# Other places in SBUF for the weights of five stretches of float32r products, a later START in mLSTM, and first weight copies on VectorE in layer 1

## The chip, the cores and the metric

The kernel runs on one core of one Trainium2 chip, in one launch. The metric is the device time of that launch in microseconds; lower is better. The core's engines are TensorE (PE, with its weight loads shown apart as PEld), VectorE (DVE), ScalarE (ACT), GpSimd (POOL) and SyncE (SP), which issues most DMA transfers.

## The reference

The reference runs four mixer layers of width 1024 over 256 tokens: two transformer layers, each with a squared-ReLU MLP, then an mLSTM mixer and a sparse-attention (NSA) mixer. Everything is float32.

```python
for layer in range(2):                      # first_block
    h = rms_norm(x, g_mix[layer])
    x = x + (even_mixer(h, ...) if layer == 0 else odd_mixer(h, ...))
    h = rms_norm(x, g_mlp[layer])
    u = einsum("bsd,df->bsf", h, w_up[layer])          # 1024 -> 4096
    x = x + einsum("bsf,fd->bsd", square(relu(u)), w_down[layer])
# second_block
x = x + mlstm_mixer(rmsnorm(x, ml_norm), ...)   # w_in 1024 -> 4096, w_out 2048 -> 1024
x = x + nsa_mixer(rmsnorm(x, nsa_norm), ...)
return rmsnorm(x, final_norm)
```

Nearly all arithmetic is in the products with the weight matrices (`w_in`, `w_out`, `w_up`, `w_down`). In the mLSTM the input projection feeds a short convolution, from which values and gates are made; in layer 1 (`odd_mixer`) 16 heads attend causally with a forget gate.

## The kernel before

**Weights in chunks.** All weight matrices are packed into one DRAM tensor of 137 chunks, each 128 partitions by 2048 float32 (1 MB), and used in order. For each chunk, `prepare` starts the DMA into `wraw` on SyncE's queue and cuts it into two float32r parts: ScalarE copies it rounded into `whi` (L124), VectorE writes the rest, `wraw - whi`, into `wlo` (L127), in halves of 1024 columns. The activations are cut the same way into pairs (`xh`, `xl`; `hh`, `hl`; `yh`, `yl`). A float32 product is then three float32r products: high by high, low by high, high by low. The ring holds three buffers of each of `wraw`, `whi` and `wlo`; two chunks are prepared ahead of the one in use (one ahead in part of layer 1).

**Two ways of multiplying.** In `gemm_tok_steps` (L199 to L201) the activations are the stationary operand, loaded with LDWEIGHTS, and a chunk's columns move, 512 at a time (256 in chunk 2): the output has tokens on the partitions. In `bank_add` (L239, L241, L242) a 128 x 128 block of the chunk is stationary and 256 tokens of the activations move; a chunk gives 16 blocks and 48 products. `gemm_feat`, `out_proj_steps`, `mlp` and the input and output projections of the mLSTM all go through `bank_add`.

**Where the operands lie.** `chunk_tiles` allocates `whi` and `wlo` aligned to LINE = 256 bytes, with SHIFT = 48 spare elements. Chunks in TOK, those that `gemm_tok_steps` uses, start 48 elements (192 bytes) into the tile, all others at 0. The activations' tiles come from `late`, which puts them 192 bytes past a multiple of 256. Chunk numbers by use: 9 to 12 layer 0's output, 13 to 28 its MLP up, 29 to 44 down; 57 to 60 layer 1's output, 61 to 76 up, 77 to 92 down; 93 to 108 mLSTM's input, 109 to 116 its output; the rest is layer 0's and layer 1's input and NSA.

**Breaks in the stream.** Between two runs of products others come in: after each MLP's up half `norm_end` (L299) makes the sum of squares, and `rstd_row` (L314) spreads the reciprocal over the partitions with four small products, a few products into the down half.

**mLSTM.** Here the order of TensorE's instructions is the order of the code (`manual_schedule`). Loop step i of `order` does `gemm_feat` of chunk 93 + i, in 8 blocks k of six products; `between[i][k]` holds what is put in ahead of block k. From step 2 on the finished banks are worked up on VectorE and ScalarE: `x_tiles` evacuates into `xi` (L761, two buffers, begun by a memset at L760), convolves (L772) and writes `xc` (L775). For each pair of x tiles, `values` (L783, 16 small products of `xi` with `bdv`) and `gates` (L790, products of `xc` and `xi`) go into TensorE's stream together. For the first pair the place is START = (4, 2): chunk 97, ahead of block 2; for the second pair (6, 4). The `bdv` tiles, two buffers, are loaded from POOL's queue (L763).

**Layer 1.** `causal_heads` works through four head pairs: scores (L515, L519), softmax (VectorE L467, ScalarE L470, VectorE L478 and L485), then `weights_T` transposes the weights on TensorE (L499) and copies them out of PSUM into `pt` (L501) with `nc.any`, which lets the scheduler choose between VectorE and ScalarE, and `pv` multiplies with the values (L528). Products of the next group's projection are put in between as fills. Only layer 1 passes `extra` to `causal_heads`.

The order of all other instructions on each engine is the scheduler's; `issue_after` holds the VectorE cuts behind some chains.

Of the kernel before, what the change touches and what calls it, by code (L numbers as in the profile page):

```python
# [10 lines left out]
F32R = mybir.dt.float32r  # L11
# [6 lines left out]
P = 128  # L18
# [7 lines left out]
PTBUFS = 2  # L26

LAG = (2, 4)
START = (4, 2)
WARM = 3  # L30
RAW = (125, 126)

TOK = {*range(9), *range(45, 57), *range(117, 121), 123, 124, 127, 128, 135, 136}


LINE = 256
SHIFT = 48
PSUM = dict(s=2, t=2, o=1)


# [31 lines left out]
def late(pool, shape, name):  # L72

    n = int(np.prod(shape))
    t = pool.tile([P, SHIFT + n], F32R, name=name, tag=name, bufs=1, align_bytes=LINE)[:, SHIFT:]
    names = "abcdefg"[:len(shape)]
# [3 lines left out]
class Builder:  # L80
# [11 lines left out]
    def begin(self):  # L92
# [4 lines left out]
        with self.tc.tile_pool(name="warm", bufs=1) as pool:  # L97
            z = pool.tile([P, 512], F32, name="zero", tag="zero")
            nc.vector.memset(z, 0.0)
            ps = self.pa.tile([P, 512], F32, name="t", tag="t", bufs=PSUM["t"])  # L100
            for i in range(WARM):
# [13 lines left out]
        self.chunk_no = 2  # L115

    def chunk_tiles(self):
        at = SHIFT if self.chunk_no in TOK else 0
        parts = [self.ring.tile([P, 2048 + SHIFT], F32R, name=n, tag=n, bufs=3, align_bytes=LINE)[:, at:at + 2048]
                 for n in ("whi", "wlo")]  # L120
        return [self.ring.tile([P, 2048], F32, name="wraw", tag="wraw", bufs=3)] + parts

# [29 lines left out]
    def single(self, tag, shape=(P, 512)):  # L152
        pool = self.pr if tag == "s" else self.pa
        return pool.tile(list(shape), F32, name=tag, tag=tag, bufs=PSUM[tag])

# [138 lines left out]
    def norm_end(self, kind, tag="t"):  # L294

        nc = self.nc
        ps = self.pa.tile([P, 512], F32, name=tag, tag=tag, bufs=PSUM[tag])
        for b in range(2):
# [10 lines left out]
    def rstd_row(self, scale=1.0):  # L309

        nc = self.nc
        ps = self.pa.tile([P, 512], F32, name="t", tag="t", bufs=PSUM["t"])
        for b in range(2):
# [93 lines left out]
    def transposed(self, t, c0, n):  # L407

        nc = self.nc
        ps = self.pa.tile([P, 2, T], F32, name="t", tag="t", bufs=PSUM["t"])  # L410
        for i in range(n):
# [75 lines left out]
            self.chain = last  # L487
        return Ls

    def weights_T(self, pool, Ls):  # L490

        nc = self.nc
        out = []

        for w, parts in ((P, (2,)), (T, (0, 1))):
            ps = self.pa.tile([P, 2, w], F32, name="t", tag="t", bufs=PSUM["t"])
            for e in range(2):
                for j, i in enumerate(parts):
                    nc.tensor.transpose(ps[:, e, j * P:(j + 1) * P], Ls[e][:, i * P:(i + 1) * P], self.ident)  # L499
            pt = pool.tile([P, 2, w], F32, name="pt", tag=f"pt{w}", bufs=PTBUFS)  # L500
            nc.any.tensor_copy(pt, ps)  # L501
            out.insert(0, pt)
        return out

# [26 lines left out]
    def causal_heads(self, pool, qk, v, vcol, tables, yh, yl, npair, extra=None, sinks=None, fills=(0, 0, 0, 0)):  # L531
        def weights(p):
            s = self.scores(qk(p), [extra(2 * p + e) for e in range(2)] if extra else None)
            kw = dict(hold=extra is not None)
            if sinks is not None:
                kw.update(nsinks=sinks[0][:, 2 * p:2 * p + 2], sinks=sinks[1][:, 2 * p:2 * p + 2])
            return self.softmax(pool, s, [tables(2 * p + e) for e in range(2)], **kw)

        ahead = [weights(0)]
        for p in range(npair):  # L540
            if p + 1 < npair:
                self.fill(fills[0])
                ahead.append(weights(p + 1))
            self.fill(fills[1 if p == 0 else 2])
            pts = self.weights_T(pool, ahead.pop(0))
            self.fill(fills[3])
            o = self.pa.tile([P, 512], F32, name="o", tag="o", bufs=PSUM["o"])
            self.pv(o, pts, v(), [vcol(p, e) for e in range(2)], True, True)
            self.split(yh[:, p], yl[:, p], o[:, :T])
# [179 lines left out]
    def mlstm(self):  # L729
# [3 lines left out]
        with tc.tile_pool(name="ml", bufs=2) as pool:  # L733
# [69 lines left out]
            with tc.manual_schedule(engines={PE}):  # L803
# [4 lines left out]
                for i, n in enumerate(order):  # L808
# [3 lines left out]
                    for n, p in ps:  # L812
                        if n is None:
                            z_tiles(i // 3, p)
                        else:

                            pair += x_tiles(n, p)
                            if n % 2:
                                at = max((order.index(n) + LAG[0], LAG[1]), START if n < 2 else (0, 0))
                                between[at[0]].setdefault(at[1], []).extend(pair[::2] + pair[1::2])  # L820
# [591 lines left out]
```

## Time and profile before

| | |
|---|---|
| timed runs | 945.35, 947.33 and 2352.52 us; median 947.33 us |
| the profiled execution | 939.13 us, of which its span (first to last instruction) 937.4 us |
| mean granted TensorE clock | 0.999 of 2.4 GHz |
| TensorE busy | 921.9 us, 98% of the span |
| VectorE, ScalarE busy | 692.2 us (74%), 553.6 us (59%) |
| DMA | 152.55 MB, mean 163 GB/s |

Busy time of TensorE counts a product from its start to its end, and products overlap: the next one starts before the last one's results are out. So the duration of a product (276 ns, say) is not what it costs; that is the distance from its start to the next start. Times of rows are microseconds from the span's start.

### The profile page before, as it was taken

How to read it: one execution, taken by the hardware profiler on the slowest of the kernel's cores; microseconds unless marked ns; L12 is line 12 of the kernel's file. 1: busy time of each engine (PE TensorE's matmuls, PEld its weight loads, DVE VectorE, ACT ScalarE, POOL GpSimd, SP SyncE). 2: the span in 40 equal slices, each digit the busy share in tenths (PEclk: the TensorE clock that was granted, in tenths of full speed). 3: DMA queues.
4: the chain of work that ended last, by engine and by line, in shares of the span. 5: the costliest groups of instructions: out<-in, count | busy, mean ns of one | idle time of the engine just before them, and what ended most of it. 6: DMA issues, size and time to landing. Idle time of an engine off the chain costs nothing.

```text
span 937.4 us, 17579 instructions
## 1 busy us (share of the span) xinstructions
PE 921.9 (98%) x7096; PEld 843.7 (90%) x7096; DVE 692.2 (74%) x1510; ACT 553.6 (59%) x1028; POOL 6.8 (1%) x16
## 2 busy tenths in 40 slices
PE   9999999999999999999999999999999999999997
PEld 6777999999998777899999999899888998888986
DVE  6997866655557787998664556978778878778994
ACT  7767656544445675566554444556645456379883
POOL 0000000000000000000000000000000000000000
PEclk9999999999999999999999999999999999999999
DMA  8723455555554342365555555544411555341311
GB/s 308 300 91 135 166 207 211 182 184 186 192 196 170 124 167 90 136 223 204 201 180 189 210 186 192 191 147 163 141 69 45 180 194 180 135 180 47 113 46 45
DMA packets 22609, 152.55 MB, mean 163 GB/s; under 512 B 2608, under 2 KB 2736, under 8 KB 4992
## 3 DMA queue, kind: packets, MB, share of 16 engines
q1 hardware_dynamic: 21744, 148.44, 44.8%
q0 software_dynamic: 784, 2.98, 0.9%
q8 instruction: 56, 0.92, 0.4%
q14 instruction: 25, 0.20, 0.1%
HBM read 150.36 MB, written 1.05 MB: 162 GB/s over the span
## 4 chain that ended last, share of the span: by engine, by line
PE 86%; DVE 6%; ACT 5%; issue 1%; DMA 1%; SPq 0%; ACTq 0%; DVEq 0%
PE g L239 19%; PE g L242 19%; PE g L241 19%; PE g L199 4%; PE g L200 4%; PE g L201 4%; DVE wlo L127 2%; PE o L528 2%; PE t L499 2%; ACT L L470 1%; ACT whi L124 1%; PE s L1140 1%; PE s L199 1%; PE s L200 1%; PE s L201 1%
## 5 line engine op out<-in xcount | busy, mean ns | idle before, releaser
L127 DVE TENSOR_TENSOR wlo<-wraw,whi 128x1024 fp32r<-128x1024 f32 (+1 forms) x274 | 324.1, 1204 | 123.7 <-ACT whi L124 123.1
L124 ACT ACTIVATE whi<-wraw 128x1024 fp32r<-128x1024 f32 (+1 forms) x274 | 277.8, 1042 | 217.9 <-PE g L241 118.3
L242 PE MATMUL g<-xh,wlo 128*128 128x256 f32 x928 | 260.3, 280 | 0.0
L239 PE MATMUL g<-xh,whi 128*128 128x256 f32 x928 | 259.0, 279 | 0.0
L241 PE MATMUL g<-xl,whi 128*128 128x256 f32 x928 | 258.5, 279 | 0.0
L239 PEld LDWEIGHTS g<-xh,whi 128*128 128x128 f32 x928 | 174.6, 188 | 2.2 <-issue 0.9
L242 PEld LDWEIGHTS g<-xh,wlo 128*128 128x128 f32 x928 | 174.6, 188 | 0.8 <-issue 0.2
L241 PEld LDWEIGHTS g<-xl,whi 128*128 128x128 f32 x928 | 174.4, 188 | 0.2
L239 PE MATMUL g<-hh,whi 128*128 128x256 f32 x512 | 142.8, 279 | 0.0
L242 PE MATMUL g<-hh,wlo 128*128 128x256 f32 x512 | 142.8, 279 | 0.0
L241 PE MATMUL g<-hl,whi 128*128 128x256 f32 x512 | 142.6, 279 | 0.0
L242 PEld LDWEIGHTS g<-hh,wlo 128*128 128x128 f32 x512 | 97.2, 190 | 0.0
L239 PEld LDWEIGHTS g<-hh,whi 128*128 128x128 f32 x512 | 96.1, 188 | 0.0
L241 PEld LDWEIGHTS g<-hl,whi 128*128 128x128 f32 x512 | 96.1, 188 | 0.0
L199 PE MATMUL g<-whi,xh 128*128 128x512 f32 x176 | 71.5, 406 | 0.4 <-ACT xh L279 0.3
L200 PE MATMUL g<-wlo,xh 128*128 128x512 f32 x176 | 70.0, 397 | 0.0
L201 PE MATMUL g<-whi,xl 128*128 128x512 f32 x176 | 68.8, 394 | 0.0
L470 ACT ACTIVATE L<-L,nm 128x128 f32<-128x128 f32 (+1 forms) x128 | 56.6, 449 | 13.0 <-DVE nm L467 12.9
L239 PE MATMUL g<-yh,whi 128*128 128x256 f32 x224 | 63.5, 284 | 0.0
L242 PE MATMUL g<-yh,wlo 128*128 128x256 f32 x224 | 62.8, 280 | 0.0
L241 PE MATMUL g<-yl,whi 128*128 128x256 f32 x224 | 62.6, 279 | 0.0
L239 PEld LDWEIGHTS g<-yh,whi 128*128 128x128 f32 x224 | 42.1, 188 | 1.4 <-issue 1.4
(354 smaller groups left out, 1373.3 us busy)
## 6 DMA issues: line engine op xcount, KB each, us to landing
wraw<-in_w SPq DMA_DIRECT2D x135, 1024.0 KB, 4.9
wraw<-in_w SPq DMA_DIRECT2D x4, 512.0 KB, 7.2
tabs<-in_tabs SPq DMA_DIRECT2D x2, 1024.0 KB, 8.9
xT<-in_x SPq DMA_DIRECT2D x4, 256.0 KB, 7.3
bdv<-in_bdv POOLq DMA_DIRECT2D x8, 128.0 KB, 2.9
mlw<-in_mlw POOLq DMA_DIRECT2D x1, 992.0 KB, 6.9
nq<-in_gf POOLq DMA_DIRECT2D x1, 512.0 KB, 3.9
out_y<-nqr SPq DMA_DIRECT2D x2, 256.0 KB, 2.1
```

The lines of the kernel that those rows point to most:

```text
L124: self.nc.scalar.activation(hi[:, s], w[:, s], AF.Copy)
L127: self.nc.vector.tensor_tensor(lo[:, s], w[:, s], hi[:, s].bitcast(F32), op=ALU.subtract)
L199: nc.tensor.matmul(ps[b][:, :n], xh, hi[:, sl], start=kt == 0, stop=False)
L200: nc.tensor.matmul(ps[b][:, :n], xh, lo[:, sl], start=False, stop=False)
L201: nc.tensor.matmul(ps[b][:, :n], xl, hi[:, sl], start=False, stop=kt == KT - 1)
L239: nc.tensor.matmul(o, hi[:, s], ah, start=bank["new"], stop=False)
L241: nc.tensor.matmul(o, hi[:, s], al, start=False, stop=False)
L242: nc.tensor.matmul(o, lo[:, s], ah, start=False, stop=last and j == 1 and i == len(acts) - 1)
L470: nc.scalar.activation(Ls[i][:, c], Ls[i][:, c], AF.Exp, bias=nm[:, b, i:i + 1], scale=-1.0, accum_out=den[:, b, i:i + 1])
L499: nc.tensor.transpose(ps[:, e, j * P:(j + 1) * P], Ls[e][:, i * P:(i + 1) * P], self.ident)
L528: nc.tensor.matmul(o[64 * e:64 * e + 64, kt * P:T], v[:, kt, c0[e]:c0[e] + 64], pts[kt][:, e], start=start and kt == 0, stop=stop and kt == 1)
L1140: nc.tensor.matmul(ps, q[:, b * P:(b + 1) * P], kst[:, g, e, o, :, :P + b * P], start=o == 0, stop=o == 1)
```

## The change

`START` goes from (4, 2) to (4, 7). `whi` and `wlo` get ROOM = 64 spare elements instead of 48, and chunks in five ranges start 56, 60, 4, 52 or 40 elements into their tile instead of at 0; TOK chunks stay at 48 and all others at 0. In layer 1, the first head pair (p = 0) of each of the two groups has its copies out of PSUM on VectorE by name instead of `nc.any`.

```diff
-START = (4, 2)
+START = (4, 7)
...
+ROOM = 64
+
+PLACES = ((range(10, 29), 56), (range(29, 45), 60), (range(59, 77), 4), (range(77, 95), 52), (range(110, 117), 40))
...
     def chunk_tiles(self):
-        at = SHIFT if self.chunk_no in TOK else 0
-        parts = [self.ring.tile([P, 2048 + SHIFT], F32R, name=n, tag=n, bufs=3, align_bytes=LINE)[:, at:at + 2048]
+        at = SHIFT if self.chunk_no in TOK else sum(n for chunks, n in PLACES if self.chunk_no in chunks)
+        parts = [self.ring.tile([P, 2048 + ROOM], F32R, name=n, tag=n, bufs=3, align_bytes=LINE)[:, at:at + 2048]
                  for n in ("whi", "wlo")]
...
-    def weights_T(self, pool, Ls):
+    def weights_T(self, pool, Ls, by=None):
...
-            nc.any.tensor_copy(pt, ps)
+            (by or nc.any).tensor_copy(pt, ps)
...
-            pts = self.weights_T(pool, ahead.pop(0))
+
+            pts = self.weights_T(pool, ahead.pop(0), self.nc.vector if extra is not None and p == 0 else None)
```

## Rows read from the trace of the kernel before

**Rows 1.** The page: busy time of each engine; engines' shares of the last chain.
```profile
PE 921.9 (98%) x7096; PEld 843.7 (90%) x7096; DVE 692.2 (74%) x1510; ACT 553.6 (59%) x1028; POOL 6.8 (1%) x16
...
PE 86%; DVE 6%; ACT 5%; issue 1%; DMA 1%; SPq 0%; ACTq 0%; DVEq 0%
```

**Rows 2.** Waits of TensorE, whole span: us in total, times, longest us.
```profile
PE o L790 <- DVE xc L775: 2.1, 1, 2.1
...
PE o L528 <- ACT pt L501: 0.9, 1, 0.9
```

**Rows 3.** L239 in six stretches: count, duration ns min/median/max, first and last start.
```profile
L239 PE MATMUL g<-xh,whi x192: 276/276/276, 122.9 to 187.8; 128*128 128x256 f32 x192
...
L239 PE MATMUL g<-hh,whi x223: 281/281/281, 200.9 to 279.3; 128*128 128x256 f32 x112
...
L239 PE MATMUL g<-xh,whi x240: 276/276/276, 405.5 to 486.8; 128*128 128x256 f32 x120
...
L239 PE MATMUL g<-hh,whi x224: 276/276/276, 499.0 to 574.8; 128*128 128x256 f32 x112
...
L239 PE MATMUL g<-xh,whi x15: 281/281/281, 728.3 to 733.2; 128*128 128x256 f32 x15
...
L239 PE MATMUL g<-yh,whi x63: 276/276/276, 746.4 to 767.5; 128*128 128x256 f32 x63
```

**Rows 4.** Timeline of TensorE, both MLPs' down halves: start, length, instruction, count.
```profile
194.98 0.63 PE L314 MATMUL t<-cst,nr 128*128 128x128 f32 x4
...
493.63 0.63 PE L314 MATMUL t<-cst,nr 128*128 128x128 f32 x4
```

**Rows 5.** L199 in layer 1 as in rows 3, and timeline of chunk 2.
```profile
L199 PE MATMUL g<-whi,xh x16: 389/389/395, 285.3 to 295.5; 128*128 128x512 f32 x16
...
20.10 0.28 PE L201 MATMUL s<-whi,xl 128*128 128x256 f32 x1
...
20.70 0.28 PE L200 MATMUL s<-wlo,xh 128*128 128x256 f32 x1
```

**Rows 6.** Timeline of mLSTM's scores; groups by form: L519's busy us, mean ns.
```profile
673.19 1.89 PE L896 MATMUL s<-xc,yk 128*128 128x256 f32 x8
...
L519 PE MATMUL s<-negc,selr 64*128 64x384 f32 x16 | 2.7, 335 | 0.0
```

**Rows 7.** Timeline of TensorE around the first and the second pair of x tiles.
```profile
604.81 1.95 PE L783 MATMUL s<-bdv,xi 128*128 128x128 f32 x16
...
609.93 0.39 PE L239 MATMUL g<-xh,whi 128*128 128x256 f32 x1
...
622.76 1.95 PE L783 MATMUL s<-bdv,xi 128*128 128x128 f32 x16
...
625.07 0.38 PE L790 MATMUL o<-xc,W 128*8 128x256 f32 x1
...
625.62 0.38 PE L239 MATMUL g<-xh,whi 128*128 128x256 f32 x1
```

**Rows 8.** Timeline of VectorE and POOL there; in brackets idle time and releaser.
```profile
608.65 0.68 DVE L775 SCALAR_TENSOR_TENSOR xc<-cu,cv 128x512 f32<-128x512 f32 x1
609.26 0.68 DVE L761 TENSOR_TENSOR xi<-g,row 128x512 f32<-128x512 f32 x1
...
610.11 0.06 DVE L760 MEMSET xi<- 128x6 f32 x1 [0.16 <-PE o L790]
...
622.25 0.68 DVE L775 SCALAR_TENSOR_TENSOR xc<-cu,cv 128x512 f32<-128x512 f32 x1
...
606.16 0.54 POOL L763 DMA_DIRECT2D bdv<-in_bdv  x1 [24.05 <-PE s L783]
```

**Rows 9.** Timeline of ScalarE and VectorE in layer 1, both groups' first pair.
```profile
334.68 0.84 ACT L501 COPY pt<-t 128x256 f32<-128x256 f32 x2
...
334.82 0.18 DVE L478 RECIPROCAL inv<-den 128x4 f32<-128x4 f32 x1 [1.12 <-ACT L L470]
...
375.26 1.01 DVE L501 COPY pt<-t 128x256 f32<-128x256 f32 x2
```

## The prediction

> **What bounds the kernel now.** I read the page first. TensorE is busy for 921.9 of 937.4 us, and 86% of the chain that ended last is TensorE's own [rows 1]. So time can go in two ways only: TensorE waits less, or its products follow each other faster. The granted clock is 0.999 of 2.4 GHz over the whole span, so no clock is to be won. Second, the waits of TensorE: the two longest are 2.1 us for VectorE in mLSTM (L790) and, after one at the very start, 0.9 us for ScalarE in layer 1 (L528) [rows 2]; they lie where the change's two other edits are. Third, the pace of the products, which "busy" hides because they overlap. I took it from the first and last start of L239 in long unbroken stretches: L239 is every third product of a bank, so the pitch from start to start is the stretch divided by three times the count less one.
>
> The reader is to see two paces for the same instruction [rows 3]. Layer 0's mlp, up: (187.8 - 122.9)/(3 x 191) = 113.3 ns. Its down half: (279.3 - 200.9)/(3 x 222) = 117.7 ns. Layer 1's mlp: up (486.8 - 405.5)/(3 x 239) = 113.4, down (574.8 - 499.0)/(3 x 223) = 113.3. mLSTM's output: the first weights (733.2 - 728.3)/(3 x 14) = 116.7, the later ones (767.5 - 746.4)/(3 x 62) = 113.4. The durations tell the same without rounding: 281 ns at the slow pace and 276 at the quick one, minimum, median and maximum alike, while VectorE, ScalarE and DMA work beside them. The step of about 4.4 ns is no noise of other engines.
>
> The two down halves are the same code on the same shapes, with their weights at the same remainder. The rows show nothing that sets them apart: the same four small L314 products break in soon after the start, for 0.63 us each time [rows 4]. One run comes out of that at the slow pace and one at the quick pace, and each keeps it to its end. I read this as two reads of TensorE, the moving operand and the next weights, that interfere or not by their phase and by where they begin. That is argued from the two paces; no row shows an address.
>
> **The change, part by part.** *Places.* `chunk_tiles` puts `whi` and `wlo` of 78 chunks at 224, 240, 16, 208 or 160 bytes past a multiple of 256 instead of at 0 (56, 60, 4, 52, 40 elements of 4 bytes); each chunk is 48 products, 3744 in all. No instruction is added, and the writes of ScalarE and VectorE and the DMA keep their sizes: the chunks in TOK sit 192 bytes off already and are written by the same two lines. The tiles grow from 2096 to 2112 elements, exactly 33 x 256 bytes; as each is aligned to 256, I take the slots as unmoved, at no cost.
>
> What can it give? Slow now among those chunks are the down half of layer 0 (16 chunks, 768 products) and one chunk at the head of mLSTM's output (48). At 4.4 ns each that is 816 x 4.4 = 3.6 us, if the new places hold the quick pace everywhere. Nothing hides it, since TensorE sets the pace, and nothing else falls late by it: ScalarE and VectorE are busy for 59% and 74% of the span [rows 1].
>
> Is there a third pace below 113.3? No row shows one. The 512-wide products take (295.5 - 285.3)/(3 x 15) = 226.7 ns, the same 0.443 ns per column at another place and with the operands' roles swapped; the 256-wide ones of chunk 2 take (20.70 - 20.10)/5 = 120 ns [rows 5]. The products of L519 read one column for all their weights, so the place of their own weights can't matter: duration less pitch is 162.7 ns at the quick pace (276 - 113.3) and 162.3 for the wide ones (389 - 226.7), so their 335 ns mean 172 ns for 384 columns, 0.449 each [rows 6]. From below the nearest row is plain float32: L896 does 256 columns in two passes in (1.89 - 0.38)/7 = 0.216 us, 108 ns a pass [rows 6]. I take 113.3 as the floor, since every float32r row stands there or above, and keep 108 and 120 as bounds.
>
> The Trainium skill speaks against this edit. By "TensorE: Matmul & The Clock Gate", section "Step-by-step: what each phase is for", TensorE has two independent read ports, and loading the next weights steals no bandwidth from the running product. By that rule a place changes nothing and this term is 0 instead of 3.6 us. The two paces of one instruction don't agree with it as it stands.
>
> *mLSTM, START (4,2) to (4,7).* The values and gates of the first two x tiles now stand ahead of chunk 97's last block instead of its third: 30 products later, 30 x 0.1133 = 3.4 us, so L783 starts at 604.81 + 3.4 = 608.2 [rows 7]. In the second pair the last gates come 625.07 - 622.76 = 2.3 us after the first L783, so here at 610.5; what they wait for ends at 608.65 + 0.68 = 609.3 [rows 7, 8]. The wait goes. The block took 609.93 - 604.81 = 5.1 us; it will take the second pair's 625.62 - 622.76 = 2.9, so 2.2 less.
>
> What is late next: the gates also free `xi`. VectorE began the third tile at 609.26 and the fourth after a wait for L790 at 610.11 [rows 8]; now the first buffer is free only at about 610.5, 1.2 us later, and behind that memset on VectorE queue the evacuation, the convolution and the cuts of two chunks. The second pair stays at (6,4). TensorE reaches it 2.2 us sooner, so its last gates want `xc` at 625.07 - 2.2 = 622.9. VectorE makes it at 622.25 + 0.68 = 622.9 if nothing moved and at 624.1 if all of the 1.2 us comes through. So 0 to 1.2 us come back as a wait at the second pair. Net gain 1.0 to 2.2; I take 1.3, nearer the low end, as VectorE runs almost without a pause there. POOL's two transfers of `bdv` wait for L783 [rows 8] and follow it by 3.4 us; their tiles are wanted at the second pair, over 10 us later. Chunk 100's weights wait for chunk 97's last product, and that comes earlier.
>
> *Layer 1, the first copies of weights on VectorE.* In the first group ScalarE does both copies, from 334.68 for 0.84 us, behind its exponentials, and TensorE waits 0.9 [rows 2, 9]. VectorE stands idle for 1.12 us before 334.82. Its own two copies in the second group take 1.01 us [rows 9]: started at 333.7 they end at 334.7, about when L528 would begin without its wait. Gain 0.85 at best. If the reciprocal and the scalings are put ahead instead, the copies end about 2 us later and it costs 1.3. In the second group VectorE does them already, so nothing changes there. I take 0.7.
>
> **Sum.** 3.6 + 1.3 + 0.7 = 5.6 us. From the profiled execution's 939.1 us that gives 933.5. The timed runs are at 945.35 and 947.33, 6 to 8 us above it. The one thing seen here that can differ by whole microseconds from run to run is the pace that a stretch falls into: 18 chunks (layer 1's output and up, or layer 1's down with mLSTM's first two) at the slow pace are 864 x 4.4 = 3.8 us, two such stretches 7.6. If that is the 6 to 8 us, places that hold the pace take them too, and the median also comes to about 934; if it is anything else, the median becomes 947.3 - 5.6 = 941.7. I say 934.
>
> **Rivals.** *The places do nothing*, and a run's pace depends on its phase alone: only 2.0 us go, 945 by the median, 937 by the profile. For it: one place, 0, shows both paces. Against: chunk 2 has another place and another pace. It is what the section of the Trainium skill named above would give.
>
> *A third pace.* At plain float32's 108 ns, 2928 products gain 5.3 and 816 gain 9.7 ns: 23.4 us, with the waits 25.4: 914 from the profile, 922 from the median. For it: the pass at 108. Against: no float32r product in the rows. It alone would make over 2%.
>
> *The new places are worse.* Chunk 2's 120 ns shows that some relation of the two operands is slower still. At 120 everywhere, 2928 x 6.7 + 816 x 2.3 = 21.5 us, less the waits 19.5: 959 from the profile, 967 from the median. The sign turns once one stretch of 18 chunks falls there (864 x 6.7 = 5.8 us, the whole sum). Against: five places would have to be bad for a clear loss.
>
> *The wait returns at the second pair in full*, VectorE then setting mLSTM's first third: 0.3 more than in my sum. It lies inside my range.
>
> **How the numbers follow.** "Faster" and "slower" mean by over 2%, about what a measurement here can tell from no change: below 928.4 or above 966.3. Quick pace held and the waits mostly gone: 0.58, between 931 and 942. Places do nothing: 0.16, 937 to 946. Third pace, whole or on some runs: 0.17, 914 to 930. Worse places: 0.09, 945 to 968. Faster takes the third pace and a sliver of the first case: 0.18. Slower needs nearly the whole of the worse places: 0.04. Same: 0.78. For 8 in 10 the range goes from 922 (108 ns, by the median) to 947 (no change); the likeliest case's own range is 931 to 942.
>
> **What would show it.** L239 in layer 0's down half should have a duration of 276 ns and 113.3 ns from start to start, and so should the other four runs; 281 anywhere says that a place doesn't hold, about 271 would be the third pace, 283 the worse one. TensorE's 2.1 us before L790 should be gone, with a shorter wait for L775 at the second pair. L528's wait for L501 should be gone, and two VectorE copies should stand before the reciprocal. The prediction is wrong if a run's pace is another than 113.3, or if the timed runs keep their distance from the profile.

## The result, and the profile after

The changed kernel is slower. Its four timed runs took 955.48 to 959.04 us, median 957.07, where the kernel before ran beside it at a median of 947.16: a ratio of 1.012, interval 1.0104 to 1.0136, about 11 us (the medians lie 9.9 apart). The prediction was 934.0 us with a range of 922 to 947; the time lies 10 us above the range's upper end. Its profiled execution took 956.27 us.

The page of the changed kernel, its busy times and shares of the last chain, to be set beside [rows 1]:

```profile
PE 938.0 (98%) x7096; PEld 860.2 (90%) x7096; DVE 693.5 (73%) x1512; ACT 553.3 (58%) x1026; POOL 6.8 (1%) x16
...
PE 88%; DVE 5%; ACT 4%; issue 1%; DMA 1%; SPq 0%; ACTq 0%; DVEq 0%
```

TensorE has the same 7096 products and is busy for 16.1 us more; the span is 17.0 us longer (954.4 for 937.4). The granted clock is 0.997. Hence the products themselves follow each other more slowly. The waits of TensorE in the changed kernel (microseconds in total, times, longest; lines have moved by 3 to 4, so L531 and L794 are L528 and L790 of before) are those of [rows 2]:

```profile
PE o L531 <- DVE pt L504: 2.4, 1, 2.4
PE g L202 <- ACT xh L282: 2.0, 1, 2.0
...
PE o L794 <- DVE xc L779: 0.2, 1, 0.2
```

The mLSTM wait fell from 2.1 to 0.2. The layer 1 wait did not go: it rose from 0.9 to 2.4, with VectorE's copy where ScalarE's was. The wait at L202 is for the first activations, at 9 us.

The stretches of L242 (L239 before) in the changed kernel, which answer to [rows 3]: count, duration in ns (min/median/max), first and last start. In order: layer 0's up and down halves, layer 1's up and down, mLSTM's output in two parts.

```profile
L242 PE MATMUL g<-xh,whi x183: 277/280/285, 125.2 to 189.9; 128*128 128x256 f32 x183
...
L242 PE MATMUL g<-hh,whi x231: 280/281/283, 202.8 to 284.5; 128*128 128x256 f32 x116
...
L242 PE MATMUL g<-xh,whi x220: 279/282/285, 414.7 to 492.8; 128*128 128x256 f32 x110
...
L242 PE MATMUL g<-hh,whi x217: 277/281/283, 510.1 to 586.7; 128*128 128x256 f32 x109
...
L242 PE MATMUL g<-xh,whi x16: 277/279/281, 744.9 to 750.1; 128*128 128x256 f32 x16
...
L242 PE MATMUL g<-yh,whi x63: 277/280/281, 763.3 to 784.9; 128*128 128x256 f32 x63
```

Read them as before: stretch over three times the count less one. Up, layer 0: (189.9 - 125.2)/(3 x 182) = 118.5 ns, where it was 113.3. Down: (284.5 - 202.8)/(3 x 230) = 118.4, where it was 117.7. Layer 1: (492.8 - 414.7)/(3 x 219) = 118.9 and (586.7 - 510.1)/(3 x 216) = 118.2, both 113.3 before. mLSTM's output: (784.9 - 763.3)/(3 x 62) = 116.1, 113.4 before. None of the five places has the quick pace. The durations show a second thing: three equal values (276/276/276) became a spread of 277 to 285. By the starts of the chunks in both traces, the three stretches of 18 or 19 chunks that lost 4.9 to 5.5 ns a product cost 4.4, 4.7 and 4.1 us, the other two 0.4 and 0.9: 14.5 in all. Layer 1 costs 1.65 more. 2.2 are lost before the first output chunk, where the first activations arrive later and TensorE's granted clock stands at 1.2 GHz from 10.3 to 13.7 us; no edit touches that part, and seven other traces of this study have such a stretch there. mLSTM gives 2.25 back at its first pair and loses 1.0 again on the way to its output: 0.3 at the second pair, the rest mostly in chunks left at place 0 (95, 96, 103, 104), which ran at 117.8 ns here.

### The profile page after: what moved, and what is told of

Read it like the earlier page. It is cut to its first block, busy times and chain, and to the rows that moved or that the text cites. A ratio compares the mean times of both kernels' runs of the same rounds, so it can differ in the third digit from the quotient of the medians.

```text
span 954.4 us, 17577 instructions
## 1 busy us (share of the span) xinstructions
PE 938.0 (98%) x7096; PEld 860.2 (90%) x7096; DVE 693.5 (73%) x1512; ACT 553.3 (58%) x1026; POOL 6.8 (1%) x16
## 4 chain that ended last, share of the span: by engine, by line
PE 88%; DVE 5%; ACT 4%; issue 1%; DMA 1%; SPq 0%; ACTq 0%; DVEq 0%
PE g L242 19%; PE g L244 19%; PE g L245 19%; PE g L202 4%; PE g L203 4%; PE g L204 4%; PE o L531 2%; DVE wlo L130 2%; PE t L502 2%; ACT L L473 1%; PE s L1144 1%; PE s L202 1%; PE s L203 1%; PE s L204 1%; PE s L886 1%
## 5 line engine op out<-in xcount | busy, mean ns | idle before, releaser
L245 PE MATMUL g<-xh,wlo 128*128 128x256 f32 x928 | 263.4, 284 | 0.0
L242 PE MATMUL g<-xh,whi 128*128 128x256 f32 x928 | 262.2, 283 | 0.0
L244 PE MATMUL g<-xl,whi 128*128 128x256 f32 x928 | 261.6, 282 | 0.0
L242 PEld LDWEIGHTS g<-xh,whi 128*128 128x128 f32 x928 | 175.0, 189 | 2.2 <-issue 0.9
L242 PE MATMUL g<-hh,whi 128*128 128x256 f32 x512 | 144.2, 282 | 0.0
L242 PEld LDWEIGHTS g<-hh,whi 128*128 128x128 f32 x512 | 96.9, 189 | 0.0
L202 PE MATMUL g<-whi,xh 128*128 128x512 f32 x176 | 72.0, 409 | 2.0 <-ACT xh L282 2.0
L242 PE MATMUL g<-yh,whi 128*128 128x256 f32 x224 | 64.1, 286 | 0.0
L473 ACT ACTIVATE L<-L,nm 128x128 f32<-128x128 f32 (+1 forms) x128 | 56.6, 448 | 12.7 <-DVE nm L470 12.6
L202 PEld LDWEIGHTS g<-whi,xh 128*128 128x128 f32 x176 | 33.5, 191 | 12.1 <-ACT xh L282 3.6
```

The costliest lines, as they stand in the source:

```text
L202: nc.tensor.matmul(ps[b][:, :n], xh, hi[:, sl], start=kt == 0, stop=False)
L242: nc.tensor.matmul(o, hi[:, s], ah, start=bank["new"], stop=False)
L244: nc.tensor.matmul(o, hi[:, s], al, start=False, stop=False)
L245: nc.tensor.matmul(o, lo[:, s], ah, start=False, stop=last and j == 1 and i == len(acts) - 1)
L473: nc.scalar.activation(Ls[i][:, c], Ls[i][:, c], AF.Exp, bias=nm[:, b, i:i + 1], scale=-1.0, accum_out=den[:, b, i:i + 1])
```

## The experiments

Numbers on chunks and places are as in the code: a place is the number of elements into the tile, and the activations lie at 48. Paces per chunk are worked out from the starts of all its products, so they have one digit more than a stretch's first and last start give. Kernels that are compared with one ratio ran on one chip beside the kernel before, whose medians there were 944.3 to 945.3 us.

### The places alone, and the two waits alone

```diff
 # p_only: the changed kernel, less
-START = (4, 7)
+START = (4, 2)
-            pts = self.weights_T(pool, ahead.pop(0), self.nc.vector if extra is not None and p == 0 else None)
+            pts = self.weights_T(pool, ahead.pop(0))
 # w_only: the changed kernel, less
-PLACES = ((range(10, 29), 56), (range(29, 45), 60), ...)
+PLACES = ()
```

> The changed kernel with its places alone: START back at (4, 2) and the first copies of layer 1 back with nc.any. If the places are the cause of the loss, the five stretches stay at 116.7 to 118.8 ns per product and the kernel is 14 to 15 us slower than before (3744 products, 2928 of them by 5 ns and 816 by 0.5 at most). If the loss comes of an interplay with the two moved waits, the stretches fall back to 113.3 ns and it is within 2 us of before.

> The changed kernel without its places (all five ranges at 0 again), with START (4, 7) and the copies on VectorE. The trace after has the mLSTM wait down from 2.1 to 0.2 us and the layer 1 wait up from 0.9 to 2.4. If these two hold by themselves: 2.2 us gained and 1.6 lost, 0.6 us faster than before, with the stretches at the paces of before (113.3 ns, or 117.8 in any one of them). If the places did all of the loss, nothing else shows.

The places alone took 955.83 us, a ratio of 1.0115 (1.0088 to 1.0142): 10.9 us slower. By the profiled executions it is 14.6 (953.68 against 939.13), the 14 to 15 that were expected; another execution of the kernel before had one more slow stretch than the first (below). The two other edits alone took 945.74, a ratio of 1.001 (0.9996 to 1.0024): nothing gained, where 0.6 less was expected. L242 with the places alone, in the two halves of layer 0 and of layer 1:

```profile
L242 PE MATMUL g<-xh,whi x190: 277/281/285, 122.7 to 189.8; 128*128 128x256 f32 x190
...
L242 PE MATMUL g<-hh,whi x230: 280/280/280, 202.8 to 283.7; 128*128 128x256 f32 x115
...
L242 PE MATMUL g<-xh,whi x231: 279/282/285, 410.9 to 492.8; 128*128 128x256 f32 x116
...
L242 PE MATMUL g<-hh,whi x232: 277/281/283, 504.8 to 586.8; 128*128 128x256 f32 x116
```

and with places of 0 and the two other edits, the two up halves:

```profile
L242 PE MATMUL g<-xh,whi x198: 276/276/276, 122.8 to 189.8; 128*128 128x256 f32 x198
...
L242 PE MATMUL g<-xh,whi x237: 276/276/276, 412.5 to 492.8; 128*128 128x256 f32 x119
```

(189.8 - 122.7)/(3 x 189) = 118.3 ns against (189.8 - 122.8)/(3 x 197) = 113.4. The slower pace comes with the places and goes with them, so nearly all of the loss is theirs. Both kernels have the larger tiles (ROOM = 64), so these are not the cause.

### A map of the places

```diff
 # map48: the kernel before, one chunk at each place in steps of four elements
+UP = [4 * i for i in range(16)]
+MIX = [0, 32, 16, 48, 8, 40, 24, 56, 4, 36, 20, 52, 12, 44, 28, 60]
+ODD = [24, 60, 0, 44, 12, 28, 52, 8, 36, 16, 4, 56, 20, 48, 32, 40]
+PLACES = tuple((range(c0 + i, c0 + i + 1), n) for c0, order in ((13, UP), (29, ODD), (61, UP[::-1]), (78, MIX))
+               for i, n in enumerate(order))
 # map8: the same, with the activations (and the TOK chunks) moved
-SHIFT = 48
+SHIFT = 8
 # map_fine, map_rest: the same as map48, in steps of one element
+PAIRS = {13 + i: (n, n) for i, n in enumerate(NEAR0)}          # 56 to 63, 0 to 7
+PAIRS |= {29 + i: (n, n) for i, n in enumerate(NEAR32)}        # 24 to 39
+PAIRS |= {61 + i: (0, n) for i, n in enumerate(STEPS)}         # whi at 0, wlo at 0, 4, ... 60
+PAIRS |= {78 + i: (n, 0) for i, n in enumerate(STEPS)}
...
+ORDERS = ((13, range(8, 24)), (29, range(40, 56)), (61, range(39, 23, -1)), (78, range(63, 47, -1)))
```

> The kernel before, with a place of its own for every chunk in four long stretches: 16 places in steps of 4 elements (16 bytes), rising in layer 0's up, falling in layer 1's up, in two mixed orders in the two down halves. Activations at 48 elements as before. If a place decides the pace, the four stretches give the same pitch for the same place: 113.3 ns at multiples of 16 elements (64 bytes), where before and the token chunks lie, and 116.7 to 118.8 at the places of the change, none of which is one. If the phase at which a stretch begins decides, the pitch goes with the stretch or with the chunk before it, and not with the place. If a third, quicker pace exists, some place shows a pitch below 113.3.

> The same map with activations and token chunks at 8 elements (32 bytes) instead of 48. If the pace goes by the weights' own place, the quick places are the same as in the run beside it (multiples of 16 elements). If it goes by the distance between weights and activations, the whole map moves by 40 elements, that is by 24 or 8 within the 64: place 24 behaves as 0 did (16 past the activations). The token products keep 226.7 ns in the second case and slow down or not with their own place in the first.

> One chunk at each place: in the first stretch places 56 to 63 and 0 to 7 in steps of one element, in the second 24 to 39 in steps of one, in the third hi at 0 and lo at 0, 4, ... 60, in the fourth hi at 0, 4, ... 60 and lo at 0. Theory (the pace goes by the distance between weights and activations in the 256 byte row, by steps wider than 4 elements): the fine steps show a smooth passage, 113.3 or 117.8 ns at 0 and 32 and within one or two elements of them, 118 to 120 ns from four elements on; a split pair takes the mean of its two places (hi and lo are loaded the same number of times), so 115 to 117 for one part away from 0. Rival 1 (only whole 4 byte multiples of some wider unit matter): single elements jump between 113.3 and 120. Rival 2 (a place between the steps of four already looked at is better than 113.3): a chunk shows under 113 ns; the price of that would be about 0.2 us a chunk for each ns below, 80 chunks.

> The kernel before with one chunk at each place that the fine map left out, in steps of one: 8 to 23 in chunks 13 to 28, 40 to 55 in 29 to 44, and once more 39 down to 24 in 61 to 76, 63 down to 48 in 78 to 93. Theory (only a few distances to the activations have the quick pace at all, those near 16 and 48 elements): nothing at 113.33 in 8 to 23 and 40 to 55; 32 quick or at 117.8, 61 quick. Rival (the quick places lie three elements apart through the whole row: 61, 0, 3, 6 go on as 9, 12, ... 58, 55): 113.33 at 9, 15, 18, 21 and at 58, 55, 52. Single steps of four (12, 24, 48) were slow, so it can't hold everywhere.

The four took 954.47, 953.31, 952.62 and 954.72 us (one execution each). Three chunks in a row of the fine map, at places 2, 3 and 4:

```profile
L248 PE MATMUL g<-xh,whi x17: 276/282/283, 163.5 to 169.2; 128*128 128x256 f32 x17
...
L248 PE MATMUL g<-xh,whi x16: 276/276/276, 169.2 to 174.3; 128*128 128x256 f32 x16
...
L248 PE MATMUL g<-xh,whi x16: 279/283/285, 174.6 to 179.9; 128*128 128x256 f32 x16
```

The middle one, one element from its neighbours, is 276 ns flat; (174.3 - 169.2)/(3 x 15) = 113.3. (The first row's 17th product is already the next chunk's.) Over all four maps, 226 chunks cover each of the 64 places at least once. Some of them, in ns a product (6, 61, 26 and 29 once settled, after some slower products):

| place | 56 | 60 | 4 | 52 | 40 | 0 | 32 | 3, 6 | 61 | 26, 29 | 48, 24, 12 |
|---|---|---|---|---|---|---|---|---|---|---|---|
| pace | 118.2-118.4 | 117.7-117.9 | 118.7-118.9 | 118.2-118.5 | 116.7 (once 117.8) | 113.3 or 117.8 | 113.3 or 117.8 | 113.3 | 113.3 | 113.3 and 118-120, once each | 120 |

The first five are those of the change, whose stretches ran at 118.3, 118.3, 118.8, 118.3 and 116.7: as the map has them, but for 0.5 ns in the second. Moving the activations from 48 to 8 moved the whole table by 40 elements (quick at 24 and 56, 120 at 8), so what counts is the distance between weights and activations, modulo 64 elements. The 120 ns at 48 are the pace of chunk 2 [rows 5], which lies there. Only 7 of 64 places showed 113.3 at all; with the activations at 48 these are 0, 3, 6 and 61, which lie 16, 19, 22 and 13 elements beyond them, and 32, 29 and 26, which lie 16, 19 and 22 short of them. Nothing ran below 113.3. With `whi` and `wlo` apart, the pace was 113.3 in one pair of places besides (0, 0) itself, `whi` at 0 and `wlo` at 32. The smooth passage that the fine map was expected to show is not there, nor a step of three through the whole row (9, 12, 58 and 55 are slow); the rival of jumps from one element to the next is what came. Multiples of 16 elements, which the first map was expected to show quick, were not all so: 16 ran at 118.5 to 120.0. Nor did a split pair take the mean of its places: most stood at 117 to 120, and `whi` is loaded twice for each load of `wlo`, not as often as the expectation had it. Paces were not one to a place: 0 and 32 have two, 34 ran at 119.8 and 116.7, and 55 once at 133.3 and once at 116.7.

### The kernel before once more

```diff
 # again: no edit
```

> The kernel before once more. The prediction put the 6 to 8 us between timed runs and the profiled one on the pace of the stretches: by that, this execution would show 113.3 and 117.8 ns in other stretches than the first profile did, if its span is 943 to 945, and the same if its span is 937. Rival (the pace is the same in each execution, and the difference is the start and the clock): 113.3 / 117.8 / 113.3 / 113.3 again whatever the span, and a later first transfer or a clock share under 0.999 where the span is longer.

It took 943.70 us, 4.6 more than the first profiled execution. L239 in the four halves:

```profile
L239 PE MATMUL g<-xh,whi x207: 276/276/276, 117.9 to 187.9; 128*128 128x256 f32 x104
...
L239 PE MATMUL g<-hh,whi x236: 281/281/281, 200.9 to 284.0; 128*128 128x256 f32 x118
...
L239 PE MATMUL g<-xh,whi x239: 276/276/276, 406.0 to 486.9; 128*128 128x256 f32 x120
...
L239 PE MATMUL g<-hh,whi x224: 281/281/281, 504.9 to 583.7; 128*128 128x256 f32 x112
```

Layer 1's down half, 276 ns in [rows 3], is at 281 here, the same kernel and the same place. Its 16 chunks make 16 x 48 x 4.4 = 3.4 of the 4.6 us. The prediction's guess about the gap between timed and profiled runs holds for most of this execution's: the same stretch of the same kernel took another pace. The rival in the expectation falls.

### The two waits one at a time

```diff
 # start_only: the kernel before, with
-START = (4, 2)
+START = (4, 7)
 # hold_split: places 3, 61, 6, 3, 61 (below), START as here, and in layer 1's first pair
-            (by or nc.any).tensor_copy(pt, ps)
+            if by is None:
+                nc.any.tensor_copy(pt, ps)
+            elif w == P:
+                nc.vector.tensor_copy(pt, ps)
+            else:
+                nc.scalar.copy(pt, ps)
```

> The kernel before with nothing but the issue of the second pair's first block moved to (4, 7). Theory: the 2.1 us wait of line 790 goes and 0.2 us comes at the second pair's first product, so 1.9 to 2.3 us less: 942.7 to 943.2 where before is at 945.0, a ratio of 0.9975 to 0.998. Rival (the time is given back further on, or the move costs as much as it saves): 944.5 to 945.5. Layer 1 and the five stretches as in before: 0.9 us of wait for pt, 113.3 / 117.8 / 113.3 / 113.3 ns and 117.8 then 113.3.

> Places 3, 61, 6, 3, 61 and the move; in layer 1's first pair the narrow copy on VectorE and the wide one on ScalarE. Theory (the copy that came late in the changed kernel stood behind the two cuts of weights on VectorE, 2.35 us, so only the wide copy's engine matters): the wait for pt is at most the 0.9 us of before, and 0.5 us or so if the two copies run side by side. Rival (the reciprocal and scalings that the first copy is now ahead of or among are what delays it): the wait stays at 2 us or more.

START alone took 944.60 against 944.96, a ratio of 0.9987 (0.997 to 1.0004): 1.2 us less, between 2.8 less and 0.4 more. The expected 1.9 to 2.3 lie within. Its trace has the wait of 0.2 us at L794 and 0.9 at L531. From the start of chunk 97 to that of chunk 100 the traces with (4, 2) take 24.1 to 25.0 us and those with (4, 7) 22.7 to 23.0, so 1.1 to 2.3 go; two of the maps, with (4, 2), took 26.2, because TensorE's granted clock fell to 1.2 GHz for 3.4 us about 1 us after the wait.

Set against the two edits together (1.001, on another chip), the copies on VectorE cost 0.0023 x 945 = 2.2 us, by both intervals anything from 0.1 to 4.3. Why, the changed kernel's timeline of TensorE and VectorE shows (start, length, what; in brackets idle time and releaser), to be read beside [rows 9]:

```profile
339.53 0.82 PE L502 MATMUL t<-cst,L 128*128 128x128 f32 x6
...
341.83 0.18 DVE L481 RECIPROCAL inv<-den 128x4 f32<-128x4 f32 x1 [1.12 <-ACT L L473]
341.93 0.39 DVE L504 COPY pt<-t 128x256 f32<-128x256 f32 x1
342.24 1.00 DVE L488 TENSOR_SCALAR L<-L,inv 128x128 f32<-128x128 f32 x4
343.15 2.35 DVE L130 TENSOR_TENSOR wlo<-wraw,whi 128x1024 fp32r<-128x1024 f32 x2
345.42 0.69 DVE L504 COPY pt<-t 128x512 f32<-128x512 f32 x1
```

The 1.12 us of idle time stayed where it was, 340.7 to 341.8. All six transposes were done at 340.4, so the copies had what they need before it began. But in VectorE's order the reciprocal stands ahead of them, and it waited for ScalarE (L473). The narrow copy came after the reciprocal, and the wide one after the scalings and behind both cuts of a chunk's weights, 2.35 us that were waiting for VectorE just there. It ends at 346.1, where L531 starts.

The wait is not all that the copies can cost. From the last product of chunk 44 to the first of chunk 57 the twelve traces with the copies as before take 87.6 to 87.8 us. The changed kernel takes 89.4 and that with place 3 everywhere (below) 89.3; two traces of the change with other places (below) take 90.9, and the two edits alone 92.1. In the last three the granted clock fell to 1.2 GHz around the end of this wait, for 3.4, 3.4 and 6.8 us. The two edits alone (the stretch and its length, busy time and count of products, granted share of 2.4 GHz, DMA's share and GB/s; then the end of the wait):

```profile
334.00:341.00 7.00, 5.36 (x31) 1.00 0.17 70
341.00:347.80 6.80, 6.02 (x24) 0.50 0.45 154
347.80:354.00 6.20, 6.20 (x43) 1.00 0.01 4
...
341.78 1.55 PE L531 MATMUL o<-pt,v 128*64 128x256 f32 x8 [2.41 <-DVE pt L504]
```

None of the twelve has a fall of the clock there. So the copies cost 1.6 us without it, and 3.2 or 4.4 with it. With the wide copy on ScalarE (935.72 us, one execution) the 2.4 us are gone:

```profile
PE o L536 <- ACT pt L509: 1.3, 2, 0.7
```

two waits of at most 0.7 us, one in each group, where the copies as before leave one of 0.8 or 0.9. So what stood ahead of the wide copy on VectorE was the cause, and of the 3.5 us from the narrow copy's start the cuts are 2.35. Splitting the copies gained little: 87.5 us from chunk 44 to 57, against 87.7.

### Steering the pace

```diff
 # kick: START (4, 7), places of 0 but for five single chunks
+PLACES = tuple((range(c, c + 1), 60) for c in (11, 30, 60, 78, 111))
 # kickmap: the same with other single chunks
+PLACES = tuple((range(c, c + 1), n) for c, n in {31: 4, 34: 36, 37: 24, 38: 60, 41: 63, 62: 4, 65: 36, 68: 8, 71: 24,
+               74: 63, 79: 16, 82: 28, 85: 4, 88: 8, 89: 4, 111: 4, 114: 36}.items())
```

> The move to (4, 7) and, in each of the five stretches, one chunk (11, 30, 60, 78, 111) at place 60, all others at 0. Theory (place 0 has two paces, and a chunk at 60 ahead of it leads into the quick one): the one chunk runs at 118 to 119 ns and costs some 0.2 us, each stretch behind it runs at 113.3 ns; the second stretch gains 14 chunks x 48 x 4.4 ns = 3.0 us and the last 0.4 to 0.9, five chunks cost 1.0, the move gains 1.9 to 2.3: 939.5 to 941 where before is at 945.0. Rival (which pace a stretch takes is chance of the execution, or set by what runs ahead of the stretch): stretches at 113.3 and 117.8 mixed, 942.5 to 946, and the pace changes with no regard to the kicked chunk.

> The move to (4, 7), all chunks at place 0 but some single ones: 31 at 4, 34 at 36, 37 and 38 at 24 and 60, 41 at 63; 62, 65, 68, 71, 74 at 4, 36, 8, 24, 63; 79, 82, 85 at 16, 28, 4, 88 and 89 at 8 and 4; 111 and 114 at 4 and 36. Theory (place 0 has two paces, each keeps itself, and which one a chunk takes is set by the phase it comes in with): behind a chunk elsewhere the pace can change, at the chunk's border and nowhere else, and within a chunk at 0 it is 113.33 or 117.77 throughout. By the earlier maps 4, 36 and 24 then 60 lead from slow to quick. Rival (the pace is the execution's or the stretch's own, from a cause outside these products): 29 to 44 stays at 117.77 at place 0 behind every one of them, 59 to 76 at 113.33.

The first took 939.98 us (935.55 to 944.55), a ratio of 0.9938 (0.9916 to 0.996), but its one trace, the slowest of its ten executions, doesn't show the reason that was expected: the chunks at 60 left quick stretches quick and slow ones slow (30 and 78). So why its timed runs are better is not shown. The second (943.13 us, one execution) has both passages. Chunks 78 and 79, 80 and 81, then 82 and 83:

```profile
L242 PE MATMUL g<-hh,whi x28: 281/281/281, 495.8 to 505.8; 128*128 128x256 f32 x28
L242 PE MATMUL g<-hh,whi x32: 276/280/285, 505.8 to 516.7; 128*128 128x256 f32 x32
L242 PE MATMUL g<-hh,whi x17: 276/276/276, 517.7 to 523.2; 128*128 128x256 f32 x17
L242 PE MATMUL g<-hh,whi x30: 276/281/283, 523.5 to 533.8; 128*128 128x256 f32 x30
```

Ahead of chunk 79 (place 16) the stretch is at 281, behind it at 276, and behind chunk 82 (place 28) at 281 again; chunks 85, 88 and 89 changed nothing, though 85 and 89 lie at 4, which was expected to lead to the quick pace. Stretches 29 to 44, this time quick from chunk 29 on, and 59 to 76 stayed quick behind every one. So place 0 has two paces, each keeps itself while nothing breaks in, and a foreign chunk can move it either way. That the pace belongs to the execution from outside is ruled out by the change at a chunk's border; which way a border leads could not be told beforehand.

### Places that were quick in the map

```diff
 # hold: START (4, 7), copies as before
+PLACES = ((range(11, 29), 3), (range(29, 45), 61), (range(59, 77), 6), (range(77, 95), 3), (range(110, 117), 61))
 # hold_all: the same, with
+PLACES = ((range(137), 3),)
 # after_hold, after_hold2: the changed kernel with hold's places (from chunk 10 on); after_all: with hold_all's
```

> The move to (4, 7) and places that single chunks of the fine map ran quick at: 3 in chunks 11 to 28 and 77 to 94, 61 in 29 to 44 and 110 to 116, 6 in 59 to 76. Theory (these places have the quick pace alone, no slow one beside it: each was entered from a chunk at 117.8 to 120 ns and still ran at 113.33): 113.33 ns in all five stretches, in every execution: 934 to 937 with a spread of some 3 us, since before's median holds 3.0 us for the second stretch and, in its common execution, 3.6 us for the fourth. Rival 1 (it was the buffer: chunks 18, 21, 24, 27 all lie in the first of three): one chunk in three at 113.33, the others at 118 to 120: 948 to 952. Rival 2 (these places have two paces as place 0 has): stretches mixed, 938 to 946.

> Place 3 for every chunk of float32r products outside the token chunks, the move to (4, 7), the copies as before. Theory (3 draws a chunk into the quick pace whatever it comes in with): 113.33 ns also in chunks 95 to 104 and 109, which ran at 117.8 with place 0 in the profile of the kernel with 3, 61, 6, 3, 61; 9 chunks of 16 x 3 products x 4.4 ns less, 1.9 us where they were slow, nothing in an execution where they were quick: 934 to 936. Rival (pulling in costs some products at 116 to 119 ns at each break, and the chunks between mLSTM's pairs are too short to settle): no difference from 935.9.

> The changed kernel with its five places replaced by 3, 61, 6, 3, 61; the move to (4, 7) and layer 1's copies on VectorE stay. Theory (the only thing that failed by much is that the change's five places have no quick pace; layer 1's copies fall behind two cuts of weights and cost 1.5 to 2.1 us): five stretches at 113.33 ns, the wait of 2.4 us for pt in layer 1, 0.2 us at the second pair; 1.5 to 2.1 us over the kernel with the same places and the copies as before (935.9), so 937.4 to 938 where before is at 945. Rival (the copies are as the prediction had them, 0.7 us gained, and w_only's 945.7 was noise): 935.2 to 935.5.

> The changed kernel with places 3, 61, 6, 3, 61 once more, for its trace. Its ten times lay between 937.7 and 947.1 though its profiled execution (937.95) ran all five stretches at 113.33 ns. Theory 1 (places 3, 61 and 6 have a slow pace of their own, which an execution can fall into at a stretch's first products, as place 0 has): if this one takes 941 or more, one or two of the five stretches stand at 116 to 120 ns, 16 to 18 chunks x 48 x 4 ns, 3 to 3.6 us each. Theory 2 (the stretches hold, the excess lies elsewhere): a late first transfer, a longer wait in layer 1, or the clock share, with the stretches at 113.33 ns.

> The changed kernel with place 3 for every chunk of float32r products outside the token chunks (layer 1's copies on VectorE stay). Theory (place 3 draws in, and of the three places in the kernel before this one 61 or 6 was what fell out in the timed executions): 113.33 ns throughout, 1.5 to 2.1 us over the kernel with place 3 everywhere and copies as before (934.6): 936 to 937, with a spread of 4 us. Rival (layer 1's copies on VectorE bring the later stretches in at another phase, and 3 falls out too): 940 to 945 with a spread of 8 us or more.

| kernel | us, median (lowest to highest) | ratio to before (interval) |
|---|---|---|
| 3, 61, 6, 3, 61, copies as before | 935.93 (935.0 to 938.2) | 0.9913 (0.9891 to 0.9936) |
| 3 everywhere, copies as before | 934.61 (932.84 to 936.65) | 0.9896 (0.9873 to 0.9918) |
| the change with 3, 61, 6, 3, 61 | 942.84 (937.69 to 947.08) | 0.999 (0.9962 to 1.0017) |
| the change with 3 everywhere | 936.87 (936.21 to 937.82) | 0.9923 (0.9902 to 0.9944) |

L242 with 3, 61, 6, 3 in the four halves, copies as before:

```profile
L242 PE MATMUL g<-xh,whi x230: 276/276/276, 110.0 to 187.9; 128*128 128x256 f32 x115
...
L242 PE MATMUL g<-hh,whi x239: 276/276/276, 200.7 to 281.7; 128*128 128x256 f32 x120
...
L242 PE MATMUL g<-xh,whi x248: 276/276/276, 404.0 to 487.9; 128*128 128x256 f32 x124
...
L242 PE MATMUL g<-hh,whi x230: 276/276/276, 499.8 to 577.6; 128*128 128x256 f32 x115
```

All four run at 113.3 ns, and in all three buffers of the ring, so the rival on the buffer falls. At the head of a stretch the chunk comes in at 119 ns and settles to 113.3 within its first 24 products; in layer 0's down half place 0, entered so, stayed at 117.8 in five of six traces. With 3 everywhere the later part of mLSTM's input follows (chunks 101 to 104; first the kernel with 3, 61, 6, then that with 3):

```profile
L242 PE MATMUL g<-xh,whi x54: 281/281/388, 630.1 to 651.8; 128*128 128x256 f32 x54
...
L242 PE MATMUL g<-xh,whi x48: 276/276/386, 634.8 to 653.8; 128*128 128x256 f32 x48
```

With place 0 these chunks ran at either pace (in the trace of START alone 101, 103 and 104 at 113.3), so it is not shown that place 3 is the reason. By its median this is the fastest kernel of the study, 1.0% under the one before; its interval overlaps that of the first row. With its places the change itself is at 936.87, inside the predicted range. The two ratios are 0.0027 apart, 2.6 us, with an interval from 0.4 less to 5.5 more; the two traces show 1.6 us for layer 1's copies, and 1.8 for mLSTM's output. For 3 is not safe either. The trace of the last kernel in the table, mLSTM's output at place 3:

```profile
L242 PE MATMUL g<-yh,whi x64: 282/283/283, 742.9 to 765.5; 128*128 128x256 f32 x64
```

(765.5 - 742.9)/(3 x 63) = 119.6: here place 3 fell to a slow pace of its own, behind an unsettled entry in chunk 111, and kept it. That is the likeliest cause of the wide spread in the table's third row, though not shown: its profiled execution (937.95) and one more (938.36) are both quick in all five stretches, while most of its timed runs lay at 940 to 947. The clock can be a part of it, not the whole: the runs of 942.70 and 942.99 us had a granted share of 0.997 like the profiled one, and 0.994 would cost at most some 2.8 us more (an estimate, 0.003 x 936). No trace of such a run exists, so it stays open which stretch fell out there.

## Why the prediction was wrong, point by point

**The step that failed is the condition on the places' term**, "3.6 us, if the new places hold the quick pace everywhere". They hold it nowhere; the term is +10.9 us by the timed runs (+14.5 by the two profiles) instead of -3.6. The mechanism fits: the pace goes by the distance between the two operands, and at one distance by how a stretch is entered. That it is two reads which meet remains argued; no row shows a read. But the mechanism was taken as a reason that a place other than 0 would be better, and nothing in the rows said so. Of the two places that the rows showed, 0 had the quick pace and one slow one, and chunk 2's had 120 ns [rows 5]. The map says how the choice lay: 57 of 64 places showed no quick pace, and 0, which was to be left, is one of the other seven. The rival "the new places are worse" held with its figure: priced at 120 ns it gave 959 from the profile, and it came to 956.27 at 116.7 to 118.8 ns, mostly where the quick pace had been. It had 0.09. The argument against it, that five places would have to be bad, counts as evidence only if a bad place is rare, and that was not known.

**The floor was right**: no float32r product ran below 113.3 ns at any of 64 places, so the "third pace" (0.17) falls. Its 108 ns were half of a record of L896 (0.216 us, [rows 6]); that such a record is two passes no row shows. **"The places do nothing"** falls too. The Trainium skill's rule behind that rival ("TensorE: Matmul & The Clock Gate", section "Step-by-step: what each phase is for": independent read ports, so that the next weights steal nothing from the running product) does not agree with these runs: the same products with the same operands' sizes took 113.3 to 120 ns by the distance of the two operands, 10.9 us over the kernel.

**START** was right in its mechanism, and its size agrees: 1.3 us net was said, 1.2 measured, with an interval that reaches past nothing, and 1.1 to 2.3 by the traces. The wait of 2.1 us fell to 0.2 at the second pair, inside the 0 to 1.2 that was allowed for. The values and gates of the first pair in the changed kernel, as [rows 7] and [rows 8]:

```profile
626.11 0.69 DVE L779 SCALAR_TENSOR_TENSOR xc<-cu,cv 128x512 f32<-128x512 f32 x1
...
626.24 1.95 PE L787 MATMUL s<-bdv,xi 128*128 128x128 f32 x16
628.11 0.38 PE L794 MATMUL o<-xc,W 128*8 128x256 f32 x1
```

`xc` is done at 626.8 and first wanted at 628.1, 1.3 us later; the prediction had 1.2 (610.5 less 609.3).

**Layer 1** went the other way: 0.7 us gained was said, 2.2 lost (1.6 to 4.4 by the traces). The step that failed is where the copies would stand. VectorE's idle time was taken as room for them; their transposes were done in time, but the reciprocal stood ahead of them and its wait for ScalarE is that idle time. The case named as the alternative (behind the reciprocal and the scalings, 1.3 us) is the nearer one, and it left out what is queued next on VectorE: two cuts of weights, held back to this very spot. It also priced the wait at its length alone. "No clock is to be won" was read from one execution's share of 0.999; in three of five traces with the longer wait the clock fell around its end.

**The gap between timed and profiled runs** was read rightly in kind: one more execution of the kernel before showed another half at the slow pace. With 3, 61, 6, 3, 61 and the copies as before it was gone: 935.0 to 938.2 over ten runs, where before ranged from 939.6 to 948.2 beside it. With the change's copies the same places ranged from 937.7 to 947.1, so it is not gone for good. Had the change named place 3, 934 would have been near (936.87); as it stood, the range should have reached over 957.

## What to carry to other kernels

Products can have paces by the distance between their two operands: before moving an operand, measure a map of single chunks at each place (one kernel, one trace) and take the new place from it, since a place not yet seen can well be worse than one that already shows the best pace, as 57 of 64 were here. Where a stretch can fall into several paces, look at more than one trace of the same kernel, and take durations that are equal in minimum, median and maximum as the sign of a settled one. When work is moved to an engine because it stands idle there, look up what ends that idle time and what is queued around it, and before a wait of TensorE is priced at its length, look in more than one trace whether the granted clock falls around its end.

## What the runs showed of the hardware

The pace of float32r products of 256 columns, with a new 128 x 128 block of weights each, lay between 113.3 and 122 ns (once 133) at a granted clock of 0.994 to 0.999 of 2.4 GHz over the span, by the distance between weights and activations modulo 64 elements (256 bytes), to the single element. It is not one pace to a distance: 0 showed 113.3 and 117.8, 3 showed 113.3 and 120, 55 showed 116.7 and 133.3. A pace keeps itself until something breaks in, and what follows then was not predictable from the rows. The quick distances seen are 16, 19 and 22 elements on either side and 13 on one. Why these, no run here shows.

TensorE's granted clock fell to 1.2 GHz around the end of a wait of 1.6 to 2.4 us, or up to 1.3 us later, in five of the twelve traces that have such a wait at layer 1's L531 or mLSTM's first pair, four times for 3.4 us and once for 6.8. At the waits of 0.9 us that stand at L531 in the other traces it did not.
